# Part of a depthwise convolution moved from VectorE to ScalarE and GpSimd

## The chip, the core and the metric

The kernel runs on one core of one Trainium2 chip. A core has five engines that run side by side, each through its own instruction stream in a fixed order: TensorE (PE in the profile, with its weight loads as PEld), VectorE (DVE), ScalarE (ACT), GpSimd (POOL) and SyncE (SP, which here only issues DMA transfers). GpSimd issues DMA transfers too. Engines wait for each other through semaphores. The metric is the device time of one execution in microseconds (us): before the change 2492.71 us, the median of three runs (2486.85 to 2494.23). Lower is better.

## The reference: what is computed

One layer of a hybrid decoder for 2048 prompt tokens and 8 decoding sequences of 4 tokens each (2080 tokens in all, 1024 channels).

```python
h = rmsnorm(x, g_pre)
proj = h @ w_in                                   # q, k, v, z_a, r, glu, z_b, g_a, g_b
# branch A: gated linear attention, 4 heads, per head:
#   S_t = diag(alpha_t) S_{t-1} + k_t^T v_t ;  o_t = q_t S_t
y_a = (head_rmsnorm(o) * silu(z_a)) @ w_a_out
# branch B: convolution
u = glu_a * sigmoid(glu_g)
ext = concat([conv_state, u], time)               # 30 earlier rows before the first token
cv = sum_j ext[t + j] * w_dw[j] + b_dw            # per channel, 31 taps
cv = silu(layernorm(cv, over channels))
y_b = (cv * silu(z_b)) @ w_b_out
x = x + (sigmoid(g_a) * y_a + sigmoid(g_b) * y_b) @ w_o
x = x + sigmoid(x @ w_pg) * (p @ w_pe)
y = rmsnorm(x, g_final)
```

The outputs are y for both kinds of token, the attention states and the last 30 rows of `ext` of each sequence. The change touches only the line with the sum over 31 taps: for each of 1024 channels, every output is the sum of 31 products of a shifted row with one weight per channel.

## The kernel before, in words

Channels lie on the 128 partitions, so 1024 channels are eight tiles c = 0 to 7, and tokens run along the free dimension. Every product with a weight matrix is made as three fp16 matmuls (high times high, high times low, low times high, the helper `mm3`, lines 203 to 208), so most of TensorE's work is on lines 206 to 208.

The program has these stages: the normed and transposed input and the forget gates (up to about 180 us); then the four attention heads, one after the other in steps of 256 prompt tokens with a last step for the 32 decode tokens (`gla_head`, 36 steps in all), with two other bodies of work beside them; then the two branches' output products with the convolution's LayerNorm; then the last products and norms. The work beside the heads is the convolution branch (`conv_channels`, one call per channel tile, called before the steps 0, 1, 5, 9, 13, 18, 22 and 27) and 24 gate projections (`gate_proj`, tile `wf` in, `fl` as PSUM tile, `ob` as result) that fill TensorE's free time.

What sets the order: the program is traced in this order, but a scheduler puts each engine's instructions into one fixed sequence, by priority and by its own estimate of when each can start. `later(BG)` around the convolution's taps gives them the lowest priority of all, so they stand where nothing else was thought to be ready. Once built, each engine runs its sequence in order: an instruction that waits holds up everything behind it on its engine.

`conv_channels(c)` first makes u for its tile: two products per block of 416 tokens (PSUM tiles `mm`), a tanh on ScalarE (`tg`, line 405) and a product on VectorE (`ue` for prompt tokens with 30 columns ahead, line 409; `us` for the 8 decode sequences, 34 columns each, line 411). `ue` has two buffers. Then come the taps (lines 424 to 436): two accumulators `acc` of 1024 prompt tokens (three buffers for them), the second with 32 more columns for the decode tokens. Per tap VectorE takes the shifted rows, multiplies by the tap's weight (one number per partition, `kvec`) and adds the accumulator: three instructions, two of 1024 columns and one of 32. Lines 437 and 438 send both accumulators to DRAM (`cv_d`) through GpSimd's queue.

In a step of `gla_head` that matters here, ScalarE empties TensorE's PSUM tiles (`qk` line 676, `v` and `zz` lines 702 and 703), makes exponentials (`kf`, `eq`), copies parts of `att`, and squares the step's result with a sum (`sq`, `ms`, line 838). GpSimd then turns `ms` into 1/sqrt by 14 small dependent instructions on 128x2 (`rsqrt` and `newton`: lines 189, 166, and three rounds of 178 to 181; below called the norm chain). VectorE multiplies by it (`zz`, line 841, waits for the chain), TensorE transposes (line 847), and ScalarE and VectorE write `at` (851, 852), which GpSimd's queue sends to `a_d`. VectorE has some twenty more short instructions per step on differences of `b` and on products with `qk` (lines 708 to 784), most of which read two tensors of SBUF.

Of the kernel before, what the change touches and what calls it, by code (L numbers as in the profile page):

```python
# [9 lines left out]
F32 = mybir.dt.float32  # L10
# [4 lines left out]
AF = mybir.ActivationFunctionType  # L15
# [4 lines left out]
P = 128  # L20
D = 1024
T = 2048
NS = 8
TS = 4
# [24 lines left out]
def mask_cols():  # L49
    """Columns of the mask for key part j of a level's r parts of x tokens, in blocks of 32 tokens."""  # L50
    cols, o = {}, 0
    for r, x in [(2, 1)] + LEVELS_S + LEVELS:
        for j in range(r - 1):
            w = UB // r * (r - 1 - j)
            cols[r, x, j] = o, w
            o += w
    return cols, o
# [11 lines left out]
RSF = -1.0 / 8192  # L69
NQ = 2  # L70
HS = 4
# [14 lines left out]
def hybrid_step(ctx: ExitStack, tc, A, O):  # L86
# [38 lines left out]

# [1 line left out]
    ident = cpool.tile([P, P], F32, name="ident")  # L127
    # small vectors, 128 channels on partitions
    vec = cpool.tile([P, 38], F32, name="vec")
# [34 lines left out]
    def newton(x, y, t, E=V):  # L164
        """y = 1/sqrt(x) / RSF, by an integer start and three Newton steps; t is scratch."""
        E.tensor_scalar(out=y.bitcast(I32), in0=x.bitcast(I32), scalar1=-0.5, scalar2=1597463007.0, op0=MULT, op1=ADD)
        gain = 1.0
        for _ in range(3):
            lim = 3.0 * gain * gain
            if E is V:  # L170
                E.tensor_tensor(out=t, in0=y, in1=y, op=MULT)
                E.tensor_tensor(out=t, in0=t, in1=x, op=MULT)
                E.scalar_tensor_tensor(out=y, in0=t, scalar=lim, in1=y, op0=SUB, op1=MULT)
            elif x.shape[-1] == 1:
                E.tensor_scalar(out=t, in0=y, scalar1=y, scalar2=x, op0=MULT, op1=MULT)
                E.tensor_scalar(out=y, in0=t, scalar1=lim, scalar2=y, op0=SUB, op1=MULT)
            else:
                E.tensor_tensor(out=t, in0=y, in1=y, op=MULT)  # L178
                E.tensor_tensor(out=t, in0=t, in1=x, op=MULT)
                E.tensor_scalar(out=t, in0=t, scalar1=lim, scalar2=None, op0=SUB)  # L180
                E.tensor_tensor(out=y, in0=y, in1=t, op=MULT)
            gain = -2.0 * gain ** 3
        return y

    def rsqrt(x, n, rows, scale, E=nc.gpsimd):
        """1/sqrt(x * scale + EPS) / RSF of a few columns; x is overwritten."""
        y = stat.tile([P, 4], F32, tag="rsq_y", name="rsq_y")[0:rows, 0:n]
# [4 lines left out]
    def load_w(src, c0, width=P, k0=0, nk=KC, pool=None):  # L192
        """Rows k0*128.. of src, columns c0.. (of each c0, side by side), in two fp16 parts."""
        c0 = [c0] if isinstance(c0, int) else c0
# [15 lines left out]
    def mm3_rows(out, lhs, rhs, nk=KC):  # L210
        """As mm3 for 32 columns of lhs: the contraction is spread over four groups of columns of the
        array, whose partial sums come out on partitions 32 g."""
        for i in range(nk // 4):
# [37 lines left out]
    def gate_proj(c, which, w):  # L251
        """One 128-channel tile of silu(z_b), or of the sigmoids of g_a, g_b, kept in DRAM."""
        d = (zz_d, ta_d, tb_d)[which]
# [11 lines left out]
    with sb_pool("pg", 2) as pg, sb_pool("p0", 2) as p0:  # L265
# [1 line left out]
        xT = [slab_hl(f"xT{k}") for k in range(KC)]  # L267
# [46 lines left out]

# [1 line left out]
        reset = pg.tile([P, TT], F16, name="reset", bufs=1)  # L316
        nc.gpsimd.memset(reset, 1.0)
        V.memset(reset[:, 0:T].rearrange("p (c t) -> p c t", t=P)[:, :, 0:1], 0.0)
        V.memset(reset[:, T:TT].rearrange("p (c t) -> p c t", t=TS)[:, :, 0:1], 0.0)
        # partitions 32 g + 0..15 carry r's first part, 32 g + 16..31 its second part  # L320
        mlo = pg.tile([P, 2], F32, name="mlo", bufs=1)
# [41 lines left out]

# [1 line left out]
    p2_ctx = ExitStack()  # L365
# [6 lines left out]
    V.tensor_copy(lmask, lml)  # L372
    # products within chunks, zero after the diagonal blocks
    atts = [p2.tile([P, 2, P], F32, name=f"att{i}") for i in range(2)]
# [12 lines left out]
    def conv_channels(c):  # L387
        """u of 128 channels, the new convolution states, and the depthwise convolution."""
        cs = c * P
# [34 lines left out]
        with later(BG):  # L424
            HT = T // 2
            QT = T // NQ
            accs = [p1.tile([P, HT + TD], F32, tag="acc", name="acc", bufs=3) for _ in range(2)]
            parts = [(accs[q * QT // HT][:, q * QT % HT:q * QT % HT + QT], lambda j, q=q: ue[:, q * QT + j:(q + 1) * QT + j]) for q in range(NQ)]
            parts.append((accs[1][:, HT:HT + TD].rearrange("p (b t) -> p b t", t=TS), lambda j: us[:, :, j:j + TS]))
            for j in range(CW):  # L430
                w1 = kvec[:, c, j:j + 1]
                for out, src in parts:
                    if j == 0:
                        V.tensor_scalar(out=out, in0=src(j), scalar1=w1, scalar2=b_dw[:, c:c + 1], op0=MULT, op1=ADD)
                    else:
                        V.scalar_tensor_tensor(out=out, in0=src(j), scalar=w1, in1=out, op0=MULT, op1=ADD)  # L436
            store(cv_d[:, c, 0:HT], accs[0][:, 0:HT])
            store(cv_d[:, c, HT:TT], accs[1])
# [4 lines left out]
    def conv_norm(a, n, bT):  # L443
        # LayerNorm of the convolution over the channels
        cv = []
# [5 lines left out]
        def total(ts, ps):  # L451
            """Sum of the tiles over channels, on every partition; the tiles' sum is left in sums[0]."""
            sums = [ln.tile([P, DB], F32, tag=f"s{i}", name=f"s{i}", bufs=1)[:, 0:n] for i in range(2)]
# [60 lines left out]

# [1 line left out]
    wpool2 = ctx.enter_context(sb_pool("wpool2", 10))  # L516
# [46 lines left out]

# [1 line left out]
    w_pg = [load_w(A["w_pg"][0], 0, D, k, 1, pool=wpool2) for k in range(KC)]  # L565
# [9 lines left out]
    with sb_pool("p4", 2) as p4:  # L575
        def tall(alloc, r, lhs, rhs, tag):
            """A product with r tokens on partitions."""
            ps = alloc()
# [61 lines left out]
def gla_head(tc, nc, A, O, h, L):  # L640
# [5 lines left out]
    wk = load_w(w_in, C_K + h * DK)  # L646
    # v's and the gate's columns side by side
    wvz = [load_w(w_in, [C_V + h * DV, C_ZA + h * DV], DV, 2 * g, 2) for g in range(4)]
# [5 lines left out]
    for a, n in GSEGS:  # L654
# [11 lines left out]
        dma(b, L["b_d"][:, h, a:a + n])  # L666
        # q (without its factor) and k, then v
        # (in blocks of 32 tokens, with room for 16 columns more)
        qk = p2.tile([P, 16, 48], F32, tag="qk", name="qk", bufs=2)
# [13 lines left out]
        def parts(t, m):  # L683
            return t.rearrange("p f (g m) -> p f g m", m=m)
        # v and the gate, tokens on partitions
        v = p2.tile([P, 2, DV], F32, tag="v", name="v", bufs=2)
# [14 lines left out]
        for c, ps in enumerate(pvz):  # L701
            S.activation(v[:, c], ps[0:ck, 0:DV], AF.Copy, scale=IS)
            S.activation(zz[:, c], ps[0:ck, DV:], AF.Tanh, scale=0.5 * IS)
            V.scalar_tensor_tensor(out=zz[:, c], in0=zz[:, c], scalar=1.0, in1=ps[0:ck, DV:], op0=ADD, op1=MULT)
        # decays from the chunk's start and to its end
        ein, qe = t2("ein"), t2("qe")
# [11 lines left out]
        S.copy(kdT[0:ck, 0:nck * P], pt[0:ck, 0:nck * P])  # L718
        # products within blocks of 32 tokens, a block's keys on its own columns of the array: the diagonal
        # and neighbours, then r parts of x tokens against the parts before them  # L720
        bb = blocks(b)
# [52 lines left out]
        if not dec:  # L774
            # a block's keys against the chunk's later blocks
            kf = keys_end(UB)
# [12 lines left out]
            for j in range(3):  # L789
                S.copy(att[j * UB:(j + 1) * UB, :, (j + 1) * UB:], ps[j * UB:(j + 1) * UB, :, 0:(3 - j) * UB])  # L790
        # outputs and states
        op_ = sm_tile()
# [18 lines left out]
        else:  # L811
            V.tensor_copy(qd.rearrange("p (s c) -> p s c", c=TD + TS)[:, :, 0:TS], qe.rearrange("p (s c) -> p s c", c=TS))
            # four sequences at a time, on columns 32 i of the array
            pq = sm_tile()[:, 0:DV]
# [18 lines left out]
            PE.matmul(po[0:ck, 0], lhsT=L["sel"], rhs=oq, start=True, stop=True)  # L833
        # norm over the head, gate, and back to channels on partitions
        ms = p2.tile([P, 2], F32, tag="ms", name="ms", bufs=2)[0:ck, 0:nck]
# [62 lines left out]
```

## Time and profile before

| | |
|---|---|
| median of three runs | 2492.71 us (2486.85 to 2494.23) |
| profiled execution, first to last instruction | 2480.5 us |
| TensorE busy | 2370.1 us, 96% |
| VectorE busy | 1684.2 us, 68% |
| ScalarE busy | 799.4 us, 32% |
| GpSimd busy | 420.6 us, 17% |
| convolution taps of 1024 columns on VectorE | 480 sums, 606.0 us |
| convolution taps of 32 columns on VectorE | 240 sums, 57.7 us |
| last tap starts at | 1426.2 us |

The profile is of one execution. A group's row reads: line, engine, operation, tile written <- tiles read, shapes, count | busy us, mean ns of one | idle us of the engine just before them, and what ended it. A wait's row reads: engine and line that waited <- what released it: us in total, times, longest. In a timeline row the first two numbers are the start and the duration in us. TensorE's matmul records overlap, so a group's busy time of it is not the time it needs; its busy share counts overlapping records once. GpSimd's durations are rough.

### The profile page before, as it was taken

The numbers are of one execution on the slowest core, as the hardware profiler recorded it, in microseconds if no ns is written. First come the engines' busy times: TensorE is split into PE (matmuls) and PEld (weight loads), VectorE is DVE, ScalarE is ACT, GpSimd is POOL, SyncE is SP. The second block draws the span as 40 slices with busy tenths as digits, with TensorE's granted clock in tenths as the row PEclk, the third lists the DMA queues.
The fourth block names the chain that finished last, engine by engine and source line by source line (L and its number), as shares of the span: only waits on it lengthen the run. The fifth ranks groups of instructions, "written<-read, shape, count | busy, mean of one in ns | idle before, by whom it ended". The sixth has DMA issues, their size and how long they took to land.

```text
span 2480.5 us, 43697 instructions
## 1 busy us (share of the span) xinstructions
PE 2370.1 (96%) x17089; PEld 1482.1 (60%) x17089; DVE 1684.2 (68%) x3841; ACT 799.4 (32%) x1969; POOL 420.6 (17%) x998
## 2 busy tenths in 40 slices
PE   3979999999999999999999999899999999999998
PEld 1445555655555555556555566466999996444444
DVE  4769997987876967968959955444588875223323
ACT  4741223232232232232242244432254443112111
POOL 1210222122222212211222221211000000010110
PEclk9999999999999999999999999999999999999999
DMA  7241112123121132111131121452454444111110
GB/s 182 89 138 24 39 45 72 27 79 68 46 75 31 41 78 75 46 48 31 42 105 60 45 69 53 125 164 87 98 146 114 118 132 159 45 56 35 49 58 34
DMA packets 187367, 187.78 MB, mean 76 GB/s; under 512 B 38619, under 2 KB 166809, under 8 KB 186648
## 3 DMA queue, kind: packets, MB, share of 16 engines
q1 hardware_dynamic: 167160, 124.28, 20.5%
q0 software_dynamic: 20000, 60.70, 6.4%
q8 instruction: 134, 2.20, 0.4%
q14 instruction: 73, 0.60, 0.1%
HBM read 124.57 MB, written 61.20 MB: 75 GB/s over the span
## 4 chain that ended last, share of the span: by engine, by line
PE 71%; DVE 11%; DMA 8%; POOL 4%; issue 4%; ACT 2%; SPq 0%; ACTq 0%; DVEq 0%; POOLq 0%
PE mm L206 13%; PE mm L207 12%; PE mm L208 12%; PE fl L206 8%; PE fl L207 8%; PE fl L208 8%; DVE acc L436 5%; DMA st<-in_w_in 2%; PE sm L800 1%; PE sm L801 1%; PE sm L802 1%; DVE w L200 1%; POOL rsq_t L178 1%; ACT w L199 1%; PE sm L610 1%
## 5 line engine op out<-in xcount | busy, mean ns | idle before, releaser
L436 DVE SCALAR_TENSOR_TENSOR acc<-ue,kvec,acc 128x1024 f32<-128x1024 f32 x480 | 606.0, 1274 | 1.4
L206 PE MATMUL mm<-xT,w 128*128 128x416 f16 (+2 forms) x1216 | 363.3, 303 | 11.4 <-DVE ue L409 5.9
L207 PE MATMUL mm<-xT,w 128*128 128x416 f16 (+2 forms) x1216 | 363.2, 303 | 0.0
L208 PE MATMUL mm<-xT,w 128*128 128x416 f16 (+2 forms) x1216 | 363.1, 303 | 0.0
L206 PE MATMUL fl<-xT,wf 128*128 128x416 f16 x960 | 328.5, 342 | 19.5 <-ACT xT L311 9.8
L207 PE MATMUL fl<-xT,wf 128*128 128x416 f16 x960 | 328.6, 342 | 0.0
L208 PE MATMUL fl<-xT,wf 128*128 128x416 f16 x960 | 328.2, 342 | 0.0
L207 PEld LDWEIGHTS <-w 128*128 128x128 f16 x2496 | 243.2, 98 | 75.0 <-issue 16.8
L206 PEld LDWEIGHTS <-w 128*128 128x128 f16 x2496 | 243.3, 98 | 61.9 <-issue 5.0
L208 PEld LDWEIGHTS <-w 128*128 128x128 f16 x2496 | 243.2, 98 | 58.8 <-issue 2.5
L208 PE MATMUL mm<-w,xT 128*128 128x512 f16 x512 | 194.8, 381 | 0.0
L206 PE MATMUL mm<-w,xT 128*128 128x512 f16 x512 | 194.7, 380 | 0.0
L207 PE MATMUL mm<-w,xT 128*128 128x512 f16 x512 | 194.7, 380 | 0.0
L206 PE MATMUL fl<-bT,w 128*128 128x208 f16 x640 | 161.7, 253 | 0.3 <-DVE t L546 0.3
L207 PE MATMUL fl<-bT,w 128*128 128x208 f16 x640 | 161.7, 253 | 0.0
L208 PE MATMUL fl<-bT,w 128*128 128x208 f16 x640 | 161.7, 253 | 0.0
L206 PE MATMUL mm<-aT,w 128*128 128x208 f16 x640 | 161.3, 253 | 0.2 <-DMA aT<-a_d 0.2
L208 PE MATMUL mm<-aT,w 128*128 128x208 f16 x640 | 161.5, 253 | 0.0
L207 PE MATMUL mm<-aT,w 128*128 128x208 f16 x640 | 161.5, 253 | 0.0
L206 PEld LDWEIGHTS <-wf 128*128 128x128 f16 x960 | 94.6, 99 | 91.0 <-issue 18.9
L207 PEld LDWEIGHTS <-wf 128*128 128x128 f16 x960 | 94.4, 98 | 88.1 <-issue 17.7
L200 DVE SCALAR_TENSOR_TENSOR w<-st,w 128x1024 f16<-128x1024 f32 x74 | 90.4, 1222 | 74.5 <-ACT w L199 74.2
(247 smaller groups left out, 4131.5 us busy)
## 6 DMA issues: line engine op xcount, KB each, us to landing
x<-in_x_prompt SPq DMA_DIRECT2D x32, 512.0 KB, 4.4
stf<-in_w_in SPq DMA_DIRECT2D x48, 256.0 KB, 6.8
st<-in_w_in SPq DMA_DIRECT2D x24, 512.0 KB, 9.8
zz_d<-ob POOLq DMA_DIRECT2D x40, 208.0 KB, 2.4
ta_d<-ob POOLq DMA_DIRECT2D x40, 208.0 KB, 2.3
cv<-cv_d SPq DMA_DIRECT2D x80, 104.0 KB, 2.2
zz<-zz_d SPq DMA_DIRECT2D x80, 104.0 KB, 2.1
tb_d<-ob POOLq DMA_DIRECT2D x40, 208.0 KB, 2.6
```

The lines of the kernel that those rows point to most:

```text
L178: E.tensor_tensor(out=t, in0=y, in1=y, op=MULT)
L199: S.activation(w[:, 0], st, AF.Copy, scale=SW)
L200: V.scalar_tensor_tensor(out=w[:, 1], in0=st, scalar=SW, in1=w[:, 0], op0=MULT, op1=SUB)
L206: PE.matmul(out, lhsT=lh, rhs=rh, start=(k == 0), stop=False)
L207: PE.matmul(out, lhsT=lh, rhs=rl, start=False, stop=False)
L208: PE.matmul(out, lhsT=ll, rhs=rh, start=False, stop=(k == nk - 1))
L436: V.scalar_tensor_tensor(out=out, in0=src(j), scalar=w1, in1=out, op0=MULT, op1=ADD)
L610: PE.transpose(pv[:, k, 0:r], src_t[0:r, (ko + k) * P:(ko + k + 1) * P], ident[0:r, 0:r])
L800: PE.matmul(po[:, c], lhsT=qe[:, cc], rhs=st_prev, start=True, stop=False)
L801: PE.matmul(po[:, c], lhsT=att[:, c], rhs=v[:, c], start=first, stop=True)
L802: PE.matmul(pu[:, c * DV:(c + 1) * DV], lhsT=kdT[:, cc], rhs=v[:, c], start=True, stop=True)
```

## The change

Two tiles of eight, c = 2 and 5 (`POOL_C`), no longer use VectorE for their prompt taps. Per quarter of 512 tokens, ScalarE makes the first product with the bias into the accumulator, then 30 products into a tile `tap` (two buffers), and GpSimd adds each to the accumulator: 8 + 240 instructions on ScalarE and 240 on GpSimd. The other six tiles keep VectorE's two sums of 1024 columns per tap.

For all eight tiles the decode tokens are treated otherwise: for each of the four token positions one product over all 31 taps of all 8 sequences (`pr`, 128x248) and one sum along the taps, then one addition of the bias: nine instructions on VectorE per tile where there were 31.

```diff
-NQ = 2
+POOL_C = (2, 5)
...
             HT = T // 2
-            QT = T // NQ
             accs = [p1.tile([P, HT + TD], F32, tag="acc", name="acc", bufs=3) for _ in range(2)]
-            parts = [(accs[q * QT // HT][:, q * QT % HT:q * QT % HT + QT], lambda j, q=q: ue[:, q * QT + j:(q + 1) * QT + j]) for q in range(NQ)]
-            parts.append((accs[1][:, HT:HT + TD].rearrange("p (b t) -> p b t", t=TS), lambda j: us[:, :, j:j + TS]))
-            for j in range(CW):
-                w1 = kvec[:, c, j:j + 1]
-                for out, src in parts:
-                    if j == 0:
-                        V.tensor_scalar(out=out, in0=src(j), scalar1=w1, scalar2=b_dw[:, c:c + 1], op0=MULT, op1=ADD)
-                    else:
-                        V.scalar_tensor_tensor(out=out, in0=src(j), scalar=w1, in1=out, op0=MULT, op1=ADD)
+
+            for i in range(TS):
+                pr = p1.tile([P, NS, CW], F32, tag="pr", name="pr", bufs=1)
+                V.tensor_tensor(out=pr, in0=us[:, :, i:i + CW], in1=kvec[:, c].unsqueeze(1).to_broadcast([P, NS, CW]), op=MULT)
+                V.tensor_reduce(out=accs[1][:, HT:].rearrange("p (b t) -> p b t", t=TS)[:, :, i], in_=pr, axis=mybir.AxisListType.X, op=ADD)
+            V.tensor_scalar(out=accs[1][:, HT:], in0=accs[1][:, HT:], scalar1=b_dw[:, c:c + 1], scalar2=None, op0=ADD)
+            if c in POOL_C:
+                QT = 512
+                for q in range(T // QT):
+                    o = q * QT
+                    out = accs[o // HT][:, o % HT:o % HT + QT]
+                    S.activation(out, ue[:, o:o + QT], AF.Identity, scale=kvec[:, c, 0:1], bias=b_dw[:, c:c + 1])
+                    for j in range(1, CW):
+                        t = p1.tile([P, QT], F32, tag="tap", name="tap", bufs=2)
+                        S.activation(t, ue[:, o + j:o + j + QT], AF.Copy, scale=kvec[:, c, j:j + 1])
+                        nc.gpsimd.tensor_tensor(out=out, in0=out, in1=t, op=ADD)
+            else:
+                for j in range(CW):
+                    w1 = kvec[:, c, j:j + 1]
+                    for q in range(2):
+                        out, src = accs[q][:, 0:HT], ue[:, q * HT + j:(q + 1) * HT + j]
+                        if j == 0:
+                            V.tensor_scalar(out=out, in0=src, scalar1=w1, scalar2=b_dw[:, c:c + 1], op0=MULT, op1=ADD)
+                        else:
+                            V.scalar_tensor_tensor(out=out, in0=src, scalar=w1, in1=out, op0=MULT, op1=ADD)
```

Lines behind the taps move down by 15 (the head's `qk` copy stands on line 691, the product with the norm on 856). The product of a tap is on line 441, GpSimd's sum on line 442, VectorE's sum on 451. The scheduler makes a new order of everything from the start of the heads on. Three places show it, all in head 0.

GpSimd, the norm chain of a step in head 0, before:

```order
L189 TENSOR_SCALAR ms_7308<-ms_7308 128x2
L166 TENSOR_SCALAR rsq_y_7312<-ms_7308 128x2
L178 TENSOR_TENSOR rsq_t_7313<-rsq_y_7312 128x2
L179 TENSOR_TENSOR rsq_t_7313<-rsq_t_7313,ms_7308 128x2
L180 TENSOR_SCALAR rsq_t_7313<-rsq_t_7313 128x2
L181 TENSOR_TENSOR rsq_y_7312<-rsq_y_7312,rsq_t_7313 128x2
```

and the chain of the same step now:

```order
L189 TENSOR_SCALAR ms_7556<-ms_7556 128x2
L166 TENSOR_SCALAR rsq_y_7560<-ms_7556 128x2
L442 TENSOR_TENSOR acc_6949<-acc_6949,tap_7001 128x512
L178 TENSOR_TENSOR rsq_t_7561<-rsq_y_7560 128x2
L442 TENSOR_TENSOR acc_6949<-acc_6949,tap_7004 128x512
L179 TENSOR_TENSOR rsq_t_7561<-rsq_t_7561,ms_7556 128x2
L442 TENSOR_TENSOR acc_6949<-acc_6949,tap_7007 128x512
L180 TENSOR_SCALAR rsq_t_7561<-rsq_t_7561 128x2
L442 TENSOR_TENSOR acc_6949<-acc_6949,tap_7010 128x512
L181 TENSOR_TENSOR rsq_y_7560<-rsq_y_7560,rsq_t_7561 128x2
```

A sum of the convolution now stands behind nearly every instruction of the chain. Counted over GpSimd's whole order, with `|` for the start of a chain, tile 2's 120 sums fall as 12 | 27 | 22 | 41 | 18 with 0, 4, 7, 4 and 18 DMA issues among them, and tile 5's as 12 | 24 | 26 | 25 | 33 with 0, 4, 8, 2 and 12. Each inner piece has 13 of the chain's instructions; the last piece of tile 2 has 7.

ScalarE, from one `qk` copy of head 0 on, before:

```order
L676 ACTIVATE qk_7344<-mm_7345 128x16x32
L765 ACTIVATE eq_7510<-eq_7510 128x384
L729 ACTIVATE kf_7534<-kf_7534 128x256
L702 ACTIVATE v_7395<-mm_7397 128x256
L703 ACTIVATE zz_7396<-mm_7397 128x256
L782 ACTIVATE eq_7538<-eq_7538 128x384
L702 ACTIVATE v_7395<-mm_7398 128x256
L703 ACTIVATE zz_7396<-mm_7398 128x256
L258 ACTIVATE ob_1705<-fl_1680 128x416
L707 ACTIVATE ein_7453<-b_7342 128x256
```

and from the same copy now:

```order
L691 ACTIVATE qk_7592<-mm_7593 128x16x32
L441 ACTIVATE tap_6992<-ue_6654,kvec_80 128x512
L441 ACTIVATE tap_6995<-ue_6654,kvec_80 128x512
L441 ACTIVATE tap_6998<-ue_6654,kvec_80 128x512
L853 ACTIVATE sq_7557,ms_7556<-sm_7544 128x256
L797 ACTIVATE eq_7786<-eq_7786 128x384
L853 ACTIVATE sq_7557,ms_7556<-sm_7544 128x256
L722 ACTIVATE ein_7701<-b_7590 128x256
L441 ACTIVATE tap_7001<-ue_6654,kvec_80 128x512
L441 ACTIVATE tap_7004<-ue_6654,kvec_80 128x512
L717 ACTIVATE v_7643<-mm_7645 128x256
L718 ACTIVATE zz_7644<-mm_7645 128x256
```

Products of the convolution, each of which needs a `tap` buffer that GpSimd has read, now stand between the copies that empty PSUM (`qk`, `v`, `zz`) and the squares that start the norm chain.

VectorE, around the step's product `qe`, before:

```order
L436 SCALAR_TENSOR_TENSOR acc_6985<-ue_6690,kvec_80,acc_6985 128x1024
L708 TENSOR_TENSOR qe_7454<-qk_7344,ein_7453 128x256
L436 SCALAR_TENSOR_TENSOR acc_6986<-ue_6690,kvec_80,acc_6986 128x1024
L436 SCALAR_TENSOR_TENSOR acc_6986<-us_6691,kvec_80,acc_6986 128x32
L436 SCALAR_TENSOR_TENSOR acc_6985<-ue_6690,kvec_80,acc_6985 128x1024
```

and around the same product now:

```order
L799 TENSOR_TENSOR eq_7786<-qk_7592,eq_7786 128x2x32
L723 TENSOR_TENSOR qe_7702<-qk_7592,ein_7701 128x256
L719 SCALAR_TENSOR_TENSOR zz_7644<-zz_7644,mm_7645 128x256
L719 SCALAR_TENSOR_TENSOR zz_7644<-zz_7644,mm_7646 128x256
L856 SCALAR_TENSOR_TENSOR zz_7384<-sm_7544,rsq_y_7560,zz_7384 128x256 x2
L726 TENSOR_TENSOR kd_7965<-b_7850 128x256
```

While tile 2's sums stand on GpSimd, VectorE's order holds no sums of the convolution, only the attention's instructions one after the other.

## The prediction

> **What bounds the kernel now.** I read the page's first part, then the busy times of one long stretch, then what TensorE waited for in it.
>
> ```profile
> span 2480.5 us, 43697 instructions
> PE 2370.1 (96%) x17089; PEld 1482.1 (60%) x17089; DVE 1684.2 (68%) x3841; ACT 799.4 (32%) x1969; POOL 420.6 (17%) x998
> ```
>
> The busiest engine is TensorE (PE), not VectorE (DVE). The convolution lies in the stretch in which the attention heads run, 180 to 1430 us; the windows view of it (columns: length, then busy us of PE, PEld, DVE, ACT, POOL, then granted clock, DMA share, GB/s):
>
> ```profile
> 180.00:1430.00 1250.00, 1219.92 (x8532) 714.60 (x8532) 1037.61 (x2163) 358.69 (x984) 283.09 (x600) 0.99 0.20 54
> ```
>
> PE idles 1250.00 - 1219.92 = 30 us there at a clock of 0.99; VectorE is busy 83% of the time. The waits of PE in the same stretch, the three longest:
>
> ```profile
> PE sm L847 <- DVE zz L841: 9.6, 8, 2.3
> PE mm L206 <- DVE ue L409: 5.9, 1, 5.9
> PE mm L206 <- DVE zz L704: 4.7, 6, 1.1
> ```
>
> So relief of VectorE can bring 30 us at the very most. The first row is not VectorE's own lateness: zz L841 waits for GpSimd's norm chain. The other two (10.6 us) are what a lighter VectorE queue could shorten. The question is then what the moved work costs where it lands.
>
> **What leaves VectorE.** Its convolution rows:
>
> ```profile
> L436 DVE SCALAR_TENSOR_TENSOR acc<-ue,kvec,acc 128x1024 f32<-128x1024 f32 x480 | 606.0, 1274 | 1.4
> L436 DVE SCALAR_TENSOR_TENSOR acc<-us,kvec,acc 128x32 f32<-128x32 f32 x240 | 57.7, 241 | 0.3
> L434 DVE TENSOR_SCALAR acc<-ue,kvec,vec 128x1024 f32<-128x1024 f32 x16 | 12.9, 808 | 0.2
> ```
>
> Two tiles take with them 120 sums at 1.274 and 4 products at 0.808: 156 us. The decode rows (240 at 0.241: 58 us) go too; in their place come 32 products and 32 reductions of 128x248. The nearest row, 0.406 for 128x256 (L728, below), prices them at 64 x 0.406 = 26 us (between 0.24 and twice that each: 15 to 52). VectorE loses some 188 us. None of it is on PE's path, so its direct worth is the 10.6 us above; ten of the stretch's 32 steps will hold the new work, so I keep two thirds: **-7 us** (0 to -11).
>
> **What ScalarE (ACT) gets**: 240 products of 128x512 with one column operand and 8 with two.
>
> ```profile
> L247 ACT ACTIVATE wf<-stf 128x512 f16<-128x512 f32 x48 | 27.5, 624 | 1.5 <-DMA stf<-in_w_in 1.5
> L487 ACT ACTIVATE th<-cv,lnh 128x208 f32<-128x208 f32 x80 | 42.5, 553 | 15.7 <-DVE bT L494 10.1 <-DVE cv L485 5.1
> L552 ACT ACTIVATE mT<-t 128x208 f16<-128x208 f32 x80 | 29.7, 371 | 107.0 <-DVE t L550 106.9
> ```
>
> The last two differ by two column operands: (553 - 371) / 2 = 91 ns each. A product takes 0.624 + 0.091 = 0.715, all of them 178 us. ScalarE is busy 359 of 1250 us, so as work this costs nothing. What costs is the wait: the product tile has two buffers, so product j+2 stands on ScalarE until GpSimd has added product j, and behind it in ScalarE's order stand the copies that empty PE's PSUM tiles (qk, v, sq, ob). If GpSimd is late, ScalarE is late by as much, and then PE, whose own order cannot be changed any more. Were ScalarE's idle time gone too, its 178 us would count in full.
>
> **What GpSimd (POOL) gets**: 240 sums of 128x512, two SBUF inputs each. No such instruction stands in the trace. The nearest rows, and the norm chain's and the stores' rows that share the queue (the last is from the view of line 189: duration min/median/max, then first and last start):
>
> ```profile
> L317 POOL MEMSET reset<- 128x2080 f16 x1 | 1.8, 1831 | 0.3 <-POOLq L886 0.3
> L106 POOL DMA_DIRECT2D a_d<-at x72 | 53.3, 740 | 164.3 <-DVE at L852 59.9 <-DVE dg L746 54.6 <-DVE eq L750 33.9
> L106 POOL DMA_DIRECT2D zz_d<-ob x40 | 23.1, 578 | 231.4 <-DVE ob L260 215.4 <-DVE dg L746 12.7 <-DVE la L351 2.3
> L189 POOL TENSOR_SCALAR ms<-ms x36: 181/184/4582, 251.0 to 1633.6; 128x2 f32<-128x2 f32 x32, 32x1 f32<-32x1 f32 x4
> ```
>
> One pass over an element costs 1831 / 2080 = 0.88 ns, 512 of them 0.45 us; a tiny sum costs 0.20 (rows below). So a sum of 512 takes 0.65 (one pass) to 1.55 (three: two reads and a write one after the other). I take two passes, **1.10**, because two operands have to be fetched. [...]
>
> The queue is not alone. GpSimd's timeline from 253 us, and VectorE's over the same time:
>
> ```profile
> 253.31 1.25 POOL L178 TENSOR_TENSOR rsq_t<-rsq_y 128x2 f32<-128x2 f32 x1
> 254.64 0.20 POOL L179 TENSOR_TENSOR rsq_t<-rsq_t,ms 128x2 f32<-128x2 f32 x1
> 254.92 2.48 POOL L180 TENSOR_SCALAR rsq_t<-rsq_t 128x2 f32<-128x2 f32 x1
> 257.49 1.21 POOL L181 TENSOR_TENSOR rsq_y<-rsq_y,rsq_t 128x2 f32<-128x2 f32 x1
> 258.78 0.19 POOL L178 TENSOR_TENSOR rsq_t<-rsq_y 128x2 f32<-128x2 f32 x1
> 259.05 0.20 POOL L179 TENSOR_TENSOR rsq_t<-rsq_t,ms 128x2 f32<-128x2 f32 x1
> ```
>
> ```profile
> 253.24 1.27 DVE L436 SCALAR_TENSOR_TENSOR acc<-ue,kvec,acc 128x1024 f32<-128x1024 f32 x1
> 254.82 2.47 DVE L436 SCALAR_TENSOR_TENSOR acc<-ue,kvec,acc 128x1024 f32<-128x1024 f32 x2
> 257.38 1.27 DVE L436 SCALAR_TENSOR_TENSOR acc<-ue,kvec,acc 128x1024 f32<-128x1024 f32 x1
> ```
>
> A 0.2 us instruction of GpSimd lasts 1.2 or 2.5 us where VectorE reads two SBUF tensors, and ends when VectorE's instruction (or back-to-back pair) ends: the two do not run together. Undisturbed, a chain step takes 0.27 from start to start, 0.08 of it a gap.
>
> Now demand against room. The norm chains come every (1633.6 - 251.0) / 35 = 39.5 us. By the new order six intervals between chains hold 27, 22, 41, 24, 26 and 25 sums (165), 29 stores and six chains of 14: 165 x (1.10 + 0.08) = 195, 6 x 14 x 0.27 = 23, 29 x 0.65 = 19, together 237 us; the room is 6 x 39.5 = 237. That is full before VectorE is counted. Its two-SBUF-input rows in the stretch, convolution aside, and zz L841:
>
> ```profile
> L200 DVE SCALAR_TENSOR_TENSOR w<-st,w 128x1024 f16<-128x1024 f32 x34 | 41.4, 1221 | 24.0 <-ACT w L199 24.0
> L767 DVE TENSOR_TENSOR eq<-qk,eq 128x192 f32<-128x192 f32 (+3 forms) x165 | 37.6, 278 | 0.8 <-ACT eq L765 0.8
> L764 DVE TENSOR_TENSOR eq<-b 128x192 f32<-128x192 f32 (+3 forms) x159 | 36.6, 279 | 0.1
> L730 DVE TENSOR_TENSOR kf<-kf,qk 128x256 f32<-128x256 f32 (+1 forms) x84 | 34.0, 405 | 0.0
> L728 DVE TENSOR_TENSOR kf<-b 128x256 f32<-128x256 f32 (+1 forms) x82 | 33.3, 406 | 0.0
> L841 DVE SCALAR_TENSOR_TENSOR zz<-sm,rsq_y,zz 128x256 f32<-128x256 f32 (+1 forms) x53 | 23.3, 479 | 71.7 <-POOL rsq_y L181 62.3 <-POOL rsq_y L176 9.3
> L781 DVE TENSOR_TENSOR eq<-b 128x192 f32<-128x192 f32 (+2 forms) x81 | 18.6, 280 | 0.0
> L784 DVE TENSOR_TENSOR eq<-qk,eq 128x192 f32<-128x192 f32 (+2 forms) x81 | 18.5, 280 | 0.0
> ```
>
> Without zz that is 220 us in 1250 / 39.5 = 31.6 steps, 7 us a step: 42 us late over the six. The pieces at the ends: the first 12 sums of each tile have an empty queue before them; 18 sums with 18 stores and half a chain need 21 + 12 + 2 + 7 = 42 of 39.5 (2 late), 33 sums with 12 stores and a chain 39 + 8 + 4 + 7 = 58 of 39.5 (18 late). **GpSimd's lateness: +62 us**, passed to PE through ScalarE (bounds: 0 with sums of 0.65, which save 108; 170 with 1.55, which add 108).
>
> No transfer is added; two move. The accumulators of tiles 2 and 5 go to DRAM after GpSimd's last sum instead of VectorE's, on GpSimd's own queue, and with three buffers for two accumulators a tile, the second half of tile 3 (and of tile 6) on VectorE waits for that store. In VectorE's order this row, with attention rows behind it, comes after the store's place by more than a step, so it bites only if GpSimd is late by about 40 us in one tile; I add nothing for it (bound: the 62 us again, for VectorE instead of ScalarE, not on top of them).
>
> The other side of the same exclusion: a VectorE instruction that comes while a sum runs waits for half of it, 0.55. The six attention rows above are 652 instructions, 20.6 a step, 113 us over ten steps if each waits; in the order they stand in runs of about three, and a run waits once: **+38 us** (0 to 113). The trace shows GpSimd held, not VectorE. [...] Were VectorE never held, the sum would be 38 us lower.
>
> **Sum**: 62 + 38 - 7 = +93 us on the profiled 2480.5, 2573.5. The median of the runs lies 12.2 above that execution's span (2492.7): **2585 us**.
>
> **Rivals.** *Faster:* GpSimd's sum costs one pass, 0.65. Then 108 us leave its demand, it keeps pace, ScalarE never stands, and VectorE's relief brings its 10.6 us and about as much from shorter waits elsewhere: 2475. For it: GpSimd is busy 283 of 1250 us only. Against: two inputs, and the full intervals above. Point: sums under 0.8 us. *No change:* the lateness is real but the double PSUM tiles and ScalarE's idle 71% swallow it: 2492. Against: PE idles 2% only, and a fixed order has no way to catch up. *Much slower:* sums of 1.55, or GpSimd starved behind VectorE's back-to-back pairs as at 254.92: 108 more, 2693. Point: a start-to-start distance of 1.6 us and more in the dense pieces.
>
> **How the numbers follow.** Forecast 0.66, faster rival 0.14, no change 0.08, much slower 0.12. The forecast's own range is 2530 to 2640. For 8 in 10 I leave out the faster rival and half of the much slower one: 2483 to 2680. A difference under 0.3% (7 us) cannot be told from none. Faster 0.15, same 0.08, slower 0.77.
>
> **What would show it.** Right: sums of 1.0 to 1.2 us whose distance is 1.4 or more; ScalarE standing at L441 for GpSimd; PE's busy share in the two pieces with sums under 0.9 while the rest of the stretch stays at 0.97; VectorE idle before attention rows that wait for nothing but a sum. Wrong: sums under 0.8, no wait at L441, or PE at 0.97 throughout. If VectorE shows no such gaps, its +38 falls; if PE's lost time is not where the sums are, the argument falls.

## The result, and the profile after

The changed kernel takes 2581.94 us (median of four runs, 2578.94 to 2584.45); the kernel before took 2492.14 us in the same comparison. The ratio is 1.0364, with a 95% interval of 1.0349 to 1.0378: slower by 90 us. The profiled execution has a span of 2580.0 us, 99.5 more than the one before; the span before lies 12 us under the median of its runs, the changed kernel's 2 under its own. In what follows, one of ten runs of e4 (2766.57 us, at a granted clock of 0.849) was in a slower state, and e4's median is that of the other nine. These are the first rows of its page of the profile:

```profile
span 2580.0 us, 44081 instructions
PE 2402.6 (93%) x17089; PEld 1491.7 (58%) x17089; DVE 1656.2 (64%) x3541; ACT 962.6 (37%) x2217; POOL 758.3 (29%) x1238
```

The span grew by 99.5 us and TensorE's busy time by 32.5, so its idle time grew by 67.0. VectorE lost only 28 us of busy time, where the instructions taken from it were worth 188 in the prediction: something has made the rest of its work longer.

The windows view tells where (columns: length, then busy us of PE, PEld, DVE, ACT, POOL, then granted clock, DMA share, GB/s). GpSimd's sums run from 485 to 749 us (tile 2) and from 1067 to 1314 us (tile 5):

```profile
480.00:560.00 80.00, 72.61 (x552) 41.73 (x551) 52.26 (x111) 49.18 (x107) 58.09 (x60) 0.96 0.13 35
560.00:640.00 80.00, 72.44 (x442) 40.09 (x441) 39.83 (x67) 45.92 (x87) 70.22 (x80) 0.94 0.30 64
640.00:700.00 60.00, 45.77 (x221) 23.08 (x220) 54.88 (x55) 23.51 (x43) 56.63 (x33) 0.86 0.13 44
700.00:780.00 80.00, 67.78 (x483) 39.66 (x481) 74.39 (x123) 29.24 (x72) 49.40 (x58) 0.94 0.20 62
780.00:860.00 80.00, 80.00 (x563) 47.79 (x561) 39.73 (x109) 25.68 (x74) 15.35 (x52) 1.00 0.16 41
860.00:1100.00 240.00, 231.87 (x1649) 135.54 (x1647) 167.43 (x367) 84.47 (x217) 71.46 (x130) 0.99 0.24 59
1100.00:1180.00 80.00, 73.08 (x493) 41.98 (x491) 44.59 (x90) 50.19 (x105) 68.53 (x79) 0.94 0.14 41
1180.00:1260.00 80.00, 65.52 (x418) 37.96 (x415) 50.27 (x69) 44.25 (x84) 70.88 (x76) 0.94 0.14 30
1260.00:1340.00 80.00, 65.94 (x468) 38.27 (x469) 77.84 (x110) 29.20 (x71) 45.23 (x51) 0.94 0.14 36
```

TensorE is busy 76% to 91% of the seven stretches with sums and 100% and 97% in the two between the tiles, of which the second has the first 33 us of tile 5's sums in it. Setting the n-th TensorE instruction of the one trace beside the n-th of the other says the same: the changed kernel is 8 us late at 480 us of the time before, 54 at 720, still 54 at 1080, 107 at 1280 and 99.5 at the end. Apart from the first 8 us, the loss lies where the sums are, about half of it in each tile.

The sums and the products, in the views of lines 442 and 441 (duration min/median/max, first and last start; then for whom the product waited):

```profile
L442 POOL TENSOR_TENSOR acc<-acc,tap x240: 1250/1278/3392, 485.4 to 1311.5; 128x512 f32<-128x512 f32 x120
...
  ACT tap L441: 139.3, 147
```

A sum lasts 1.25 us at the least and, by its row on the page, 1.46 in the mean; ScalarE stands 139 us before products whose buffer is not free. And these are VectorE's own convolution sum, four attention rows and `zz` in the groups of the changed kernel (before, the first five took 1.274, 0.279, 0.280, 0.406 and 0.405):

```profile
L451 DVE SCALAR_TENSOR_TENSOR acc<-ue,kvec,acc 128x1024 f32<-128x1024 f32 x360 | 483.5, 1367 | 1.6
L782 DVE TENSOR_TENSOR eq<-qk,eq 128x192 f32<-128x192 f32 (+3 forms) x196 | 65.4, 384 | 1.2 <-ACT eq L780 1.2
L779 DVE TENSOR_TENSOR eq<-b 128x192 f32<-128x192 f32 (+3 forms) x196 | 59.8, 351 | 0.0
L743 DVE TENSOR_TENSOR kf<-b 128x256 f32<-128x256 f32 (+1 forms) x100 | 47.8, 478 | 0.0
L745 DVE TENSOR_TENSOR kf<-kf,qk 128x256 f32<-128x256 f32 (+1 forms) x100 | 47.4, 474 | 0.0
L856 DVE SCALAR_TENSOR_TENSOR zz<-sm,rsq_y,zz 128x256 f32<-128x256 f32 (+1 forms) x68 | 29.9, 478 | 139.3 <-POOL rsq_y L181 128.7 <-POOL rsq_y L176 10.6
```

The first five read two tensors of SBUF. The convolution sum has become 7% longer in the mean, the attention rows 17% to 38%. The last takes one of its tensors from PSUM; it kept its 0.478 (before 0.479). In the timeline VectorE's side of this reads as follows; the row of three `eq` products lasts 2.83 us, beside two sums of GpSimd with a step of its norm chain between them:

```profile
1240.46 2.83 DVE L782 TENSOR_TENSOR eq<-qk,eq 128x192 f32<-128x192 f32 x3
```

```profile
1240.22 1.45 POOL L442 TENSOR_TENSOR acc<-acc,tap 128x512 f32<-128x512 f32 x1
1241.63 0.31 POOL L179 TENSOR_TENSOR rsq_t<-rsq_t,ms 128x2 f32<-128x2 f32 x1
1241.90 1.32 POOL L442 TENSOR_TENSOR acc<-acc,tap 128x512 f32<-128x512 f32 x1
```

Where VectorE has little but its own convolution sums to do, the two engines take turns. GpSimd's timeline, VectorE's and ScalarE's in the worst stretch:

```profile
662.77 24.18 POOL L442 TENSOR_TENSOR acc<-acc,tap 128x512 f32<-128x512 f32 x12
```

```profile
658.73 15.41 DVE L451 SCALAR_TENSOR_TENSOR acc<-ue,kvec,acc 128x1024 f32<-128x1024 f32 x7
```

```profile
666.48 0.72 ACT L441 ACTIVATE tap<-ue,kvec 128x512 f32<-128x512 f32 x1 [1.48 <-POOL acc L442]
...
686.27 0.64 ACT L717 ACTIVATE v<-mm 128x256 f32<-128x256 f32 x2
```

Twelve sums of 1.27 take 24.18 us and seven of VectorE's sums of 1.27 take 15.41, one of each every 2.0 to 2.2 us, and ScalarE stands about 1.5 us before most of its products. The copy of `v` out of PSUM comes only when the run is over, at 686.27.

### The profile page after: what moved, and what is told of

Read it like the earlier page. It is cut to its first block, busy times and chain, and to the rows that moved or that the text cites. A ratio compares the mean times of both kernels' runs of the same rounds, so it can differ in the third digit from the quotient of the medians.

```text
span 2580.0 us, 44081 instructions
## 1 busy us (share of the span) xinstructions
PE 2402.6 (93%) x17089; PEld 1491.7 (58%) x17089; DVE 1656.2 (64%) x3541; ACT 962.6 (37%) x2217; POOL 758.3 (29%) x1238
## 4 chain that ended last, share of the span: by engine, by line
PE 59%; DVE 15%; POOL 9%; DMA 7%; issue 6%; ACT 3%; SPq 1%; DVEq 0%; POOLq 0%; ACTq 0%
PE mm L206 10%; PE mm L208 10%; PE mm L207 10%; PE fl L207 7%; PE fl L208 7%; PE fl L206 7%; POOL acc L442 5%; DVE acc L451 5%; DMA st<-in_w_in 1%; DMA x<-in_x_prompt 1%; DVE eq L782 1%; DVE w L200 1%; POOL rsq_t L178 1%; DVE eq L779 1%; SPq L103 1%
## 5 line engine op out<-in xcount | busy, mean ns | idle before, releaser
L451 DVE SCALAR_TENSOR_TENSOR acc<-ue,kvec,acc 128x1024 f32<-128x1024 f32 x360 | 483.5, 1367 | 1.6
L206 PE MATMUL mm<-xT,w 128*128 128x416 f16 (+2 forms) x1216 | 370.8, 310 | 14.7 <-DVE zz L719 10.5
L442 POOL TENSOR_TENSOR acc<-acc,tap 128x512 f32<-128x512 f32 x240 | 350.3, 1460 | 76.5 <-ACT tap L441 67.7
L207 PE MATMUL mm<-xT,w 128*128 128x416 f16 (+2 forms) x1216 | 370.5, 309 | 0.0
L208 PE MATMUL mm<-xT,w 128*128 128x416 f16 (+2 forms) x1216 | 370.1, 309 | 0.0
L206 PE MATMUL fl<-xT,wf 128*128 128x416 f16 x960 | 332.1, 346 | 31.9 <-DVE ob L260 16.1
L207 PE MATMUL fl<-xT,wf 128*128 128x416 f16 x960 | 331.8, 346 | 0.0
L208 PE MATMUL fl<-xT,wf 128*128 128x416 f16 x960 | 331.4, 345 | 0.0
L441 ACT ACTIVATE tap<-ue,kvec 128x512 f32<-128x512 f32 x240 | 170.8, 719 | 147.7 <-POOL acc L442 139.3
L206 PE MATMUL mm<-aT,w 128*128 128x208 f16 x640 | 161.2, 253 | 0.5 <-DMA aT<-a_d 0.5
L207 PE MATMUL mm<-aT,w 128*128 128x208 f16 x640 | 161.4, 253 | 0.0
```

The costliest lines, as they stand in the source:

```text
L206: PE.matmul(out, lhsT=lh, rhs=rh, start=(k == 0), stop=False)
L207: PE.matmul(out, lhsT=lh, rhs=rl, start=False, stop=False)
L208: PE.matmul(out, lhsT=ll, rhs=rh, start=False, stop=(k == nk - 1))
L441: S.activation(t, ue[:, o + j:o + j + QT], AF.Copy, scale=kvec[:, c, j:j + 1])
L442: nc.gpsimd.tensor_tensor(out=out, in0=out, in1=t, op=ADD)
L451: V.scalar_tensor_tensor(out=out, in0=src, scalar=w1, in1=out, op0=MULT, op1=ADD)
```

## The experiments

Three explanations of the loss stood against each other. *Capacity and hand-over:* GpSimd's own time fills its queue, ScalarE stands for it, and TensorE stands for ScalarE. *Lock:* GpSimd and VectorE exclude each other when both read SBUF, whatever the queues hold. *Chain:* the heads' norm chains stand behind the sums. The kernel before ran in every comparison; its median was 2486.17, 2487.91 and 2485.35 us in those of e1 to e4, e5 to e8 and e9 to e12. Where I compare across them, I take each kernel's distance from the kernel before of its own comparison. Every edit also lets the scheduler make a new order; the number of sums between norm chains is given where it matters. Where a run leaves sums out, its results are wrong and only its time is of use.

**The decode edit alone (e1).**

```diff
-POOL_C = (2, 5)
+POOL_C = ()
```

> Only the decode half of the change: no channel tile goes to ScalarE and GpSimd, all eight have products and one sum for the decode tokens. My theory (the loss is GpSimd's sums alone): VectorE loses some 30 us of work that lies off TensorE's path, so 2480 to 2492 us. Rival (the decode edit, with its 32 reductions, carries a part of the 90 us): above 2500 us.

Measured: 2477.06 us, ratio 0.9968 (0.9955 to 0.9981), 9.1 us less than before and 3 us under my bracket. The products and reductions took what the row of 128x256 had let expect:

```profile
L430 DVE TENSOR_TENSOR pr<-us,kvec 128x248 f32<-128x248 f32 x32 | 12.9, 402 | 0.3 <-ACT us L400 0.3
L431 DVE TENSOR_REDUCE acc<-pr 128x8 f32<-128x248 f32 x32 | 12.7, 396 | 0.0
```

The decode half of the change is a small gain. The moved taps therefore cost 89.8 + 9.1 = 99 us, and that is what the other runs have to explain.

**The sums on VectorE (e2).**

```diff
-nc.gpsimd.tensor_tensor(out=out, in0=out, in1=t, op=ADD)
+V.tensor_tensor(out=out, in0=out, in1=t, op=ADD)
```

> ScalarE's 248 products stay, and so does their two-buffer hand-over; the 240 sums of 128x512 go from GpSimd to VectorE, where two SBUF inputs of 512 should take 0.65 us (half of 1.27 for 1024). My theory (GpSimd's price, and the lock with VectorE, are the loss): 2480 to 2505 us. Rival (ScalarE's queue: its products and the hand-over stand between the copies that empty PSUM, whoever sums): 2550 us or more.

Measured: 2505.3 us, ratio 1.0080 (1.0067 to 1.0093): 0.3 us over the upper end of what I expected, 28 us over e1. A sum took 0.684, and ScalarE stood for VectorE now:

```profile
L442 DVE TENSOR_TENSOR acc<-acc,tap x240: 668/684/712, 480.1 to 1221.0; 128x512 f32<-128x512 f32 x120
...
  ACT tap L441: 80.2, 55
```

ScalarE's products and their hand-over alone do not explain 99 us. That they cost 28 here, where VectorE does the sums, I can't split further.

**Half the width of each sum (e3).**

```diff
-nc.gpsimd.tensor_tensor(out=out, in0=out, in1=t, op=ADD)
+nc.gpsimd.tensor_tensor(out=out[:, 0:256], in0=out[:, 0:256], in1=t[:, 0:256], op=ADD)
```

> GpSimd adds only the first 256 of 512 columns of each product (the other half of the sums is left out); ScalarE's products, the number of sums and the hand-over stay. A sum should fall from 1.27 to 0.65-0.70 us. My theory (demand against room in the dense pieces, with the lock held half as long): most of the loss goes, 2490 to 2520 us. Rival ScalarE's queue: 2550 us or more, since its 248 products stay. Rival lock alone (VectorE is held by 118 us in sum, half of it stays): about 2535 us.

Measured: 2503.14 us, ratio 1.0068 (1.0054 to 1.0082), 26 us over e1.

```profile
L442 POOL TENSOR_TENSOR acc<-acc,tap x240: 713/727/2005, 484.9 to 1141.2; 128x256 f32<-128x256 f32 x120
...
  ACT tap L441: 27.2, 49
```

A sum of half the columns lasts 0.727, 57% of the whole, and three quarters of the loss are gone, though the order was as dense as in the changed kernel (up to 46 sums between two chains, where that had 41). Both capacity and lock allow this. But 0.727 is under the 0.8 us at which my faster rival should have set in, and the kernel is still slower than before.

**GpSimd kept busy without reading SBUF (e4, e10).** Both leave the sums out and let GpSimd fill the product tile instead, so that ScalarE still waits for it:

```diff
-nc.gpsimd.tensor_tensor(out=out, in0=out, in1=t, op=ADD)
+nc.gpsimd.memset(t.bitcast(F16), 0.0)              # e4: 1024 and 240 elements
+nc.gpsimd.memset(t.bitcast(F16)[:, 0:240], 0.0)
...
+nc.gpsimd.memset(t.bitcast(U8)[:, 0:1424], 0.0)    # e10: one fill
```

> Each sum is replaced by two GpSimd fills of the product tile, 1024 and 240 f16 elements (0.93 + 0.27 us and a gap: 1.28 us, the undisturbed length of a sum); they read no SBUF tensor, and the sums are left out. GpSimd's time stays, the two-input reads go. Theory capacity (GpSimd's undisturbed length against the room): a good part of the loss stays, 2530 to 2560 us. Theory lock (the two-input reads of VectorE and GpSimd exclude each other, which stretches the sum from 1.27 to 2.2 us and VectorE's rows by 118 us in sum): 2485 to 2510 us, and VectorE's attention rows are back at 0.28 and 0.41 us. If the rows of VectorE stay at 0.37 to 0.48 us, a fill locks as well and the run does not tell the two apart.

> As e4 (fills of the product tile in place of the sums, no SBUF tensor read), but one fill of 1424 one-byte elements, with GpSimd's order closer to the changed kernel's: 27, 24, 31, 22, 14 and 24, 17, 26, 27, 26 between chains, where e4 had about 20. If a fill costs 0.88 ns an element whatever its type, it lasts 1.26 us, the undisturbed length of a sum. Theory lock: 2480 to 2500 us, as e4. Theory density (what e4 took away was the dense pieces, not the lock): 2520 us or more.

Measured: e4 2485.89 us, ratio 1.0001 (0.9990 to 1.0011); e10 2476.78 us, ratio 0.9965 (0.9953 to 0.9978), 3 us under its bracket. The view of e10's line 442, VectorE's groups, one row of its timeline and one of the windows:

```profile
L442 POOL MEMSET tap<- x240: 1274/1284/1311, 439.1 to 1181.8; 128x1424 uint8 x120
...
  ACT tap L441: 82.2, 127
```

```profile
L779 DVE TENSOR_TENSOR eq<-b 128x192 f32<-128x192 f32 (+3 forms) x196 | 45.7, 279 | 0.3 <-PE sm L753 0.3
L782 DVE TENSOR_TENSOR eq<-qk,eq 128x192 f32<-128x192 f32 (+3 forms) x196 | 44.7, 278 | 1.2 <-ACT eq L780 1.2
L743 DVE TENSOR_TENSOR kf<-b 128x256 f32<-128x256 f32 (+1 forms) x100 | 40.6, 406 | 0.0
L745 DVE TENSOR_TENSOR kf<-kf,qk 128x256 f32<-128x256 f32 (+1 forms) x100 | 40.4, 404 | 0.0
```

```profile
567.71 0.69 DVE L782 TENSOR_TENSOR eq<-qk,eq 128x192 f32<-128x192 f32 x3
```

```profile
440.00:560.00 120.00, 119.98 (x841) 71.63 (x839) 40.20 (x126) 80.53 (x163) 109.16 (x138) 1.00 0.19 50
```

This settles the first question. In e10 a fill is recorded as long as an undisturbed sum, 1.284 against 1.278 in the median, ScalarE makes all its products and stands 82 us for GpSimd, and the kernel takes as long as e1, which has none of this (2476.78 and 2477.06). GpSimd's queue is about as full: from 440 to 560 us it is busy 91% of the time (109.16 us) and TensorE 100%, where the changed kernel has 89% and 82% from 1180 to 1260 us, and 94% and 76% from 640 to 700, with sums there that last 1.46 us in the mean of all 240. No fill was stretched (1311 at the most) and VectorE's rows are back at 0.28 and 0.40; three `eq` products in a row take 0.69 beside a fill, where the changed kernel had 2.83. What costs time is that the sums read SBUF while VectorE does: the row of line 779, with two SBUF inputs, takes 0.279 in the mean of e10, whose fills only write SBUF, and 0.351 in the changed kernel. Three reserves: e10's densest piece held 31 fills, where the changed kernel has one of 41 sums; back to back a fill follows a fill after 1.22 us, an undisturbed sum a sum after 1.35, so that a tap took GpSimd a tenth less; and e10's order on every engine is one of its own.

**One tile instead of two (e5).**

```diff
-POOL_C = (2, 5)
+POOL_C = (2,)
```

> Only channel tile 2 goes to ScalarE and GpSimd; tile 5 is back on VectorE; the decode edit stays. The order of GpSimd's sums of tile 2 between the norm chains is the same as in the changed kernel (12, 27, 22, 41, 18). If each tile costs its own part in place (TensorE loses some 45 us around each tile): halfway between the decode-only kernel and the changed one, 2515 to 2540 us. If the second tile only pays because the first left GpSimd late: 2560 us or more; if the loss needs both tiles: under 2495 us.

Measured: 2546.25 us, ratio 1.0232 (1.0216 to 1.0247), 67 us over e1 and 6 above my bracket. Set beside the trace before, e5 is 51 us late at 720 us of the time before, where the changed kernel is 54, so tile 2 alone does that. Tile 5's sums, back on VectorE, run from 1047 to 1157 us and add nothing lasting (45 us late at 1080, 44 at 1250). The last 20 us come after 1250 (64 at the end), where GpSimd has no sums; what makes them stays open.

**A deeper hand-over (e6), and its control (e9).** Both keep the products in f16; e6 has four buffers, which take the room of two in f32, and e9 two.

```diff
-t = p1.tile([P, QT], F32, tag="tap", name="tap", bufs=2)
+t = p1.tile([P, QT], F16, tag="tap", name="tap", bufs=4)    # e9: bufs=2
```

> The product tile has four buffers in place of two (kept in f16, since SBUF has no room for four in f32; the sums between chains are as dense as before, up to 46). Theory hand-over (ScalarE stands 139 us for GpSimd because it is only two products ahead, and what stands behind it makes TensorE late): the standing falls under 70 us and the time to 2540 us or less. Theory lock (GpSimd and VectorE exclude each other; a deeper hand-over only moves the wait): 2565 to 2590 us.

> The control of e6: the product tile in f16 as there, but with two buffers as in the changed kernel (sums between chains 12, 29, 22, 45, 12 and 13, 24, 25, 27, 31). e6 came out 26 us under the changed kernel with a sum of 1.16 us at least instead of 1.25. If the depth of the hand-over did that: 2572 to 2585 us here. If the shorter sum did it: 2550 to 2562 us.

Measured: e6 2555.68 us, ratio 1.0272 (1.0256 to 1.0287); e9 2561.42 us, ratio 1.0305 (1.0291 to 1.0319). The sums' view in e6, then in e9, with ScalarE's wait:

```profile
L442 POOL TENSOR_TENSOR acc<-acc,tap x240: 1142/1160/3991, 483.3 to 1271.0; 128x512 f32<-128x512 f32 x120
...
  ACT tap L441: 88.9, 111
```

```profile
L442 POOL TENSOR_TENSOR acc<-acc,tap x240: 1140/1160/2913, 481.6 to 1271.7; 128x512 f32<-128x512 f32 x120
...
  ACT tap L441: 119.7, 145
```

Both theories missed e6's 2556. The control tells why: with an f16 operand a sum is 0.12 us shorter, and that is worth 14 us (distance from before: +90 in the changed kernel, +76 in e9). Two more buffers take 31 us of standing from ScalarE and are worth 8 us (+68 in e6), with up to 46 sums between two chains in e6 and 45 in e9. The hand-over is a small part.

**Without VectorE's own sums (e7, and e8 as its base).** Both leave out the sums of every tile whose taps are on VectorE, so that only the attention's and other rows are left there.

```diff
-                        else:
-                            V.scalar_tensor_tensor(out=out, in0=src, scalar=w1, in1=out, op0=MULT, op1=ADD)    # e8: POOL_C = () as well
```

> The changed kernel without VectorE's 360 sums of the other six tiles (they are left out, their first products stay); ScalarE's and GpSimd's work and its order between the chains stay (13, 28, 22, 37, 20 and 17, 25, 24, 26, 21, 7). To be compared with e8, the same omission in the decode-only kernel. Theory A (the loss arises where GpSimd's sums take turns with VectorE's 1.27 us sums, 2.2 us a pair): the difference to e8 is 40 us or less, GpSimd's sums average under 1.33 us. Theory B (the attention rows of VectorE that wait out a GpSimd sum, and GpSimd's 1.27 us against its room): the difference stays at 70 us or more.

> The decode-only kernel without VectorE's sums of all eight tiles (left out): the base for e7. VectorE is not what bounds it, so 2455 to 2477 us.

Measured: e7 2507.48 us, ratio 1.0079 (1.0064 to 1.0094); e8 2459.18 us, ratio 0.9888 (0.9872 to 0.9905). The difference is 48 us, between the two brackets. VectorE's `eq` products in e7 are as long as in the changed kernel (line 780 here), and GpSimd's sums shorter, 1.325 in the mean instead of 1.46:

```profile
L780 DVE TENSOR_TENSOR eq<-qk,eq 128x192 f32<-128x192 f32 (+3 forms) x196 | 64.8, 382 | 1.6 <-ACT eq L778 1.6
```

```profile
L442 POOL TENSOR_TENSOR acc<-acc,tap 128x512 f32<-128x512 f32 x240 | 318.0, 1325 | 85.4 <-ACT tap L441 50.9 <-ACT acc L438 26.1
```

So about half of the loss needs VectorE's own sums, which take turns with GpSimd's; that it is because they leave VectorE little time to catch up is argued, not shown. The other half arises without them, on a VectorE that is busy only 47% of the time (1182.4 us), where its other rows wait out GpSimd's sums as before.

**The norm chains on VectorE (e11), and the same with the decode edit alone (e12).**

```diff
-rs = rsqrt(ms, nck, ck, 1.0 / DV)
+rs = rsqrt(ms, nck, ck, 1.0 / DV, V)    # e12: POOL_C = () as well
```

> The changed kernel with the attention heads' norm chains (14 tiny instructions each) on VectorE, so that they no longer queue behind GpSimd's sums; VectorE gets 500 instructions of 0.06 to 0.1 us. Route chain (TensorE waits for zz, zz for a chain that stands behind sums): 2545 us or less. Route ScalarE (the copies that empty PSUM stand behind a product that waits for a buffer) and VectorE's held rows: 2560 us or more, about the same as the changed kernel.

> A candidate for a faster kernel: the decode edit alone (e1), and the heads' norm chains on VectorE, where a chain takes some 2 us instead of the 4 to 10 us that it takes on GpSimd while VectorE's two-input instructions run. TensorE waited 9.6 us for zz in the kernel before, so 2462 to 2475 us; if VectorE's queue, now 35 us longer, is where the chain waits instead: 2477 us or more.

Measured: e11 2594.76 us, ratio 1.0443 (1.0429 to 1.0458); e12 2477.18 us, ratio 0.9961 (0.9948 to 0.9975). A chain step in e11, and the same in e12:

```profile
L171 DVE TENSOR_TENSOR rsq_t<-rsq_y 128x2 f32<-128x2 f32 (+2 forms) x117 | 33.7, 288 | 2.9
```

```profile
L171 DVE TENSOR_TENSOR rsq_t<-rsq_y 128x2 f32<-128x2 f32 (+2 forms) x117 | 18.2, 156 | 2.6
```

The queue behind the sums is not what costs: with the chains off it the kernel is 109 us over the one before, not 90, since the steps now wait for the sums on VectorE (0.288 instead of 0.156, where I had expected 0.06 to 0.1). And e12 is no better than e1: the two best kernels here that compute the whole result are equal, 2477 us.

**Held time beside lost time.** For every run I added up how much longer VectorE's rows, convolution sums aside, lasted than the same rows of its base (for each line: count times the difference of the means; the counts are equal). The base is e1, for e7 it is e8, for e11 it is e12.

| run | VectorE's rows held, us | time over its base, us |
|---|---|---|
| e10, fills | 6 | 0.5 |
| e4, two fills | 5 | 9 |
| e2, sums on VectorE | 2 | 28 |
| e3, half sums | 38 | 26 |
| e7, no VectorE sums | 75 | 48 |
| e5, one tile | 54 | 67 |
| e6, f16, four buffers | 96 | 77 |
| e9, f16, two buffers | 75 | 85 |
| the changed kernel | 104 | 99 |
| e11, chains on VectorE | 128 | 118 |

The time lost goes with the time held, within some 27 us either way. It is no equation: e2 loses 28 us with nothing held, and VectorE's own convolution sums, left out of the table, were held another 35 us in the changed kernel and 2 in e7, so that e7 lost 48 of 77 and the changed kernel 99 of 140. That VectorE's held rows are the way by which the lock reaches TensorE fits this table, but is not shown alone: GpSimd's sums and ScalarE's standing grow with the same cause, and no run has the one without the other.

## Why the prediction was right, and where not

It said 2585 us and a span of 2573.5; measured were 2581.94 and 2580.0. The kind of loss came out (GpSimd's sums cost far more than VectorE's relief brings, in the stretches where they stand), and so did the exclusion behind the smaller of its two large terms. The larger one failed, and that the total fits to 3 us is luck. The span was forecast 6.5 us short, and the 12.2 us added from span to median, where the changed kernel has 2, made up for that.

- *What bounds the kernel, and relief of VectorE (-7).* Right. The decode edit gave -9.1. In e10 VectorE has all the relief of the change and the sums are left out, and it gains nothing over e1: 1519.7 us of VectorE or 1664.6, the time is the same.
- *The price of a sum, 1.10.* Too low: 1.25 at the least, 1.278 in the median, 1.46 in the mean. 256 columns take 0.727 and 512 take 1.278, which is 2.15 ns a column and a fixed 0.18 us. My two passes at 0.88 ns came to 1.76 ns a column.
- *GpSimd's lateness, +62, passed on by ScalarE.* This is the step that failed. It took demand against room as what decides. e10 keeps GpSimd about as busy (91% of a dense stretch, where the changed kernel has 89% and 94%), and ScalarE stands 82 us at line 441; it costs nothing. ScalarE standing there, which I named as a sign that I was right, is no sign of loss. Only the part of the 62 that the lock made (VectorE's two-input rows holding GpSimd, 7 us a step or 42 in six) can have counted; in the trace the sums were held (1.460 - 1.278) x 240 = 44 us.
- *VectorE held by the lock, +38 (0 to 113).* Right in kind, mis-sized. No row of before shows VectorE held, and that a row would wait for half a sum, 0.55, was my estimate. The six attention rows that the term counts were held 61 us, between its 38 and its upper bound, which had each row wait. Dividing by three, because "they stand in runs of about three, and a run waits once", does not hold: at 1240.46 a run of three lasts 2.83 us instead of 0.69, while GpSimd goes through two sums and a chain step, and two of the three wait, 1.42 and 1.29 us long. The term also left out rows: the others with two SBUF inputs (`kd`, `qe`, `wf`, `pr` and more) make up most of the way from the 61 to the table's 104, and VectorE's own convolution sums were held another 35.
- *The stores, nothing.* Right: the lines with which VectorE begins an accumulator, 431 and 449, waited 0.1 and 0.0 us in all.
- *The signs.* TensorE's share under 0.9 in the pieces with sums came out in four of seven stretches; the other three have 0.91. In the rest of the heads' stretch it is 0.97 and more, but for 0.94 from 1340 to 1400 us. A distance of 1.4 us and more between sums came out, too (in the mean 2.2 in tile 2, 2.1 in tile 5), but tells little: e10's fills stand 1.7 and 1.6 apart, at no loss. VectorE idle before attention rows did not: a row that is held shows as a longer row, with no idle time before it.
- *The rivals.* The faster one's point, sums under 0.8 us, was itself wrong: e3 has 0.727 and is 17 us slower than before. The much slower one's point, a distance of 1.6 us and more, was passed (2.2 in the run at 662.77) without its 2693; as e10's distances say, that point does not tell how much is lost.

Two errors of opposite sign made the total fit: 62 where a full queue alone cost nothing, 38 where the lock held VectorE's rows 104 us, its own sums aside.

## What to carry to other kernels

Here work handed from VectorE to GpSimd was not off VectorE: GpSimd's sums read SBUF, and of VectorE's remaining rows the attention rows with two SBUF inputs became 17% to 38% longer in the mean, while `zz`, with one of its tensors in PSUM, stayed at 0.478 us. In another kernel ask first which rows of the first kind remain, and take as an estimate of the upper bound that each that meets such a GpSimd instruction waits it out, as two of three did at 1240.46 (1.42 and 1.29 us long beside sums of 1.45 and 1.32). Look for that wait in the durations, comparing one form's mean between two traces, since here no idle time and no wait showed it. To tell a full queue from such an exclusion, let the helper engine do something equally long that reads nothing (here e10's fill of 1.284 us, at no loss).

## What the runs showed of the hardware

- A sum of GpSimd over two SBUF tensors and a sum of VectorE over two took turns at 2.0 to 2.2 us a pair, less than the 1.27 + 1.27 that they last alone. Neither shows idle time: from 655 to 683 us VectorE is busy 27.68 us of 28.00 and GpSimd 27.20, so the waiting is inside the recorded durations.
- GpSimd's fill goes by elements and not by bytes: 1024 of f16 took 0.952 us, 1424 of one byte 1.284, some 0.9 ns an element both times.
- A third of the longer span is busy time of TensorE and not idle time (32.5 of 99.5 us), at least in part because its matmuls are slower. In 640 to 700 us, where it is busy 76%, the granted clock is 0.86 and the matmul of 128x416 takes 0.364 us, against 0.340 before:

```profile
L206 PE MATMUL fl<-xT,wf 128*128 128x416 f16 x29 | 10.6, 364 | 4.1 <-DVE ob L260 4.1
```

```profile
L206 PE MATMUL fl<-xT,wf 128*128 128x416 f16 x141 | 47.9, 340 | 1.1 <-DVE ob L260 1.1
```

The granted clock goes with TensorE's gaps in the nine stretches of the windows view above: 0.86 where it is busy 76%, 0.94 to 0.96 where it is busy 82% to 91%, 0.99 and 1.00 where it is busy 97% and 100%. That the gaps lower the clock, so that a wait of TensorE costs more than its own length, fits these numbers, but no run shows it alone: from 1340 to 1400 us it is busy 94% at a clock of 1.00.
